# A two-layer decoder trunk on one core: six chunks transposed by VectorE instead of TensorE, and a new order of the first loads

## The chip, the cores and the metric

The kernel runs on one NeuronCore of a Trainium2 chip. The core has a matrix engine (TensorE, PE in the profile, with its weight loads as PEld), a vector engine (VectorE, DVE), an activation engine (ScalarE, ACT), a general engine (GpSimd, POOL) and a queue engine (SyncE, SP). SP, ACT and POOL issue DMA transfers. The metric is the device time of one execution in microseconds (us), the median of several.

## What is computed

The input x has 256 rows of 2048 floats. Two layers follow one another, each with a mixing half and a feed-forward half:

```python
h = rms_norm(x, mix_norm[l]);  proj = h @ w_in[l]          # q | k | v | u,v of the gating unit | gates
branch_a = sliding_window_attention(q, k, v, sinks[l]) @ w_attn_branch[l]
branch_b = chunked_sgu(gelu(uv), ...) @ w_sgu_branch[l]
x = x + (gates[:, :2048] * branch_a + gates[:, 2048:] * branch_b) @ w_out[l]
h2 = rms_norm(x, ffn_norm[l])
x = x + (silu(h2 @ w_gate[l]) * (h2 @ w_up[l])) @ w_down[l]     # inner width 5632
```

All arrays are 32-bit floats and the result has to keep that precision. The weights of both layers are read once.

## The kernel before, in words

**A product in three parts.** TensorE multiplies in a reduced format (fp32r). So each operand is split in a high part (a copy rounded to fp32r) and a low part (the value minus the high part), and a product is high x high + low x high + high x low. `Stream.split` (L217) does this for a weight tile: ACT writes `whi` (L225), DVE writes `wlo` (L226). `add_product` (L306) issues the matmuls (L314, L315).

**Weight stream.** The weights go through in entries. An entry is a tile `raw` of 256 rows by 512 columns (512 KB) for two blocks of 128 rows of x, twelve matmuls in all. SP loads the tiles (`Stream.load`, L196, L202; the first tile in two halves, L205) into five buffers, so a load waits until the tile five entries before has been split. Each of `whi` and `wlo` has four buffers. `Stream.next` (L230) asks for a tile up to seven entries ahead and splits up to four ahead (three in the first ten entries).

**Pairs.** Two column blocks that multiply the same x are taken together as a pair, in which one unit is multiplied with seven products in the place of eight (Winograd's form of Strassen). Its seven entries (tags P1 to P7, the head) are mixed with the last six entries of the pair before; for that some weight tiles are subtracted from one another on DVE (L213), and PSUM blocks are kept and joined (L336 to L342). A pair that follows a change of x is ordered by unit: all that uses unit 1, then unit 2, then unit 3.

**Units.** What stands on the left of a product has to be transposed: 512 columns of x (or of a hidden activation) become a unit, `uh` and `ul`, four 128x256 blocks each. `transposed` (L393) makes a unit, in one of two ways. With `on_pe`, TensorE transposes eight 128x128 blocks into PSUM (L425), and ACT and DVE split them from there (L411 and L416 with a scale, L407 and L408 without). Otherwise `turn` (L376) lets DVE transpose 32x32 blocks in place (L383, one instruction per 128 rows, into the tile `box`), and sixteen DMAs of 32 KB gather the blocks into a tile `tt` (L388); ACT and DVE split that one. The DMAs go out from POOL, or from SP where the caller says so.

**What sets the order.** TensorE's order is written by hand. After every two blocks `tick` (L246) counts a slot and runs what is due: `after(n, fn)` (L243) books fn n slots on. In `turn` the second transposition and the gathers come a slot after the first; in `transposed` the split comes six and seven slots on (plus `late`). DVE's instructions in a slot are kept behind the last `wlo` or subtraction (`tc.issue_after`). Beyond such bonds the order on DVE, ACT, POOL and SP is a planner's, which plays the program through with modelled durations.

**The places that the change touches.** `residual` (L849) adds a product to x and, where a norm follows, makes that norm's units (`nxt.unit`, L863) and sums of squares (L864); before, the last unit went over TensorE three slots on. `hidden` (L940) makes a chunk of the feed-forward activation; 11 chunks are done in rounds of 4, 4 and 3, and the last chunk of each round went over TensorE (L953, L954). `product_pair` (L368) calls both when a pair ends.

**The start.** SP loads x in chunks of 512 columns, two DMAs each (L258), with weight tiles between them as `LOAD_BY` (L49) says: tiles for 1, 3, 4 and 4 entries after chunks 1 to 4. POOL makes the identity and a mask, and loads small tables: `cs` and `sn` (L539, L540), `vrows` (L545 to L547), and `gn` and `snk` through `bcast` (L281). TensorE transposes all four units of the first norm, in slots 0, 1, 3 and 5. The squares of x (`Norm.squares`, L491, on ACT) are booked for slots 3 to 6 (L527), but the planner may put them earlier, since nothing binds them.

Of the kernel before, what the change touches and what calls it, by code (L numbers as in the profile page):

```python
# [45 lines left out]
Q_TURN = 7  # L46
Q_FIRST = 17
Q_STEP = 5
LOAD_BY = (1, 3, 4, 4)  # L49
FIRST_PART = [[(("kv", 0),), (("q", 0),)] + early + [(("v", 0),), (("v", 1),), (("gate", 1), ("u", 0)), (("u", 1), ("gate", 2)),  # L50
                                                  (("gate", 3), ("gate", 4))]
              for early in ([(("q", 1),), (("gate", 0),)], [(("q", 1), ("gate", 0))])]
# [5 lines left out]
def hybrid_trunk(ctx: ExitStack, tc: tile.TileContext, x, mix_norm, w_in, q_norm, k_norm, sinks,  # L58
# [129 lines left out]
    class Stream:  # L188
# [28 lines left out]
        def split(self, upto):  # L217
            while len(self.parts) < min(upto, len(entries)):
                e = entries[len(self.parts)]
                raw = self.raws[e["src"]]  # L220
                hi = wsp.tile([P, 2, CW], F32R, tag="hi", name=nm("whi"))
                lo = wsp.tile([P, 2, CW], F32R, tag="lo", name=nm("wlo"))
                one = len(self.parts) < 2
                for i in ([slice(0, 1), slice(1, 2)] if one else [slice(0, 2)]):
                    nc.scalar.activation(hi[:, i, :], raw[:, i, :], AF.Copy)  # L225
                    self.last = nc.vector.tensor_tensor(out=lo[:, i, :], in0=raw[:, i, :], in1=hi[:, i, :].bitcast(F32),  # L226
                                            op=ALU.subtract)
                self.parts.append((hi, lo))
# [49 lines left out]
    neg_half = const.tile([P, 24], F32, name="neg_half")  # L278
    nc.gpsimd.memset(neg_half, -0.5)

    def bcast(dst, row):  # L281
        nc.gpsimd.dma_start(dst, row.unsqueeze(0).to_broadcast([P, row.shape[0]]))


    def rsqrt(dst, src, n):
# [90 lines left out]
    def turn(dst, src, queue):  # L376


        box = turned.tile([P, 4, 4, NT, B], F32, tag="box", name=nm("box"))
        iv = src.rearrange("p t (k j c) -> p t k j c", j=4, c=B)  # L380

        def blocks(t):
            nc.vector.transpose(box[:, :, :, t, :].rearrange("p j k r -> p k j r"), iv[:, t])  # L383

        def gather():
            for j in range(4):
                for i in range(4):
                    queue.dma_start(dst[j * B:(j + 1) * B, i], box[i * B:(i + 1) * B, j])  # L388

        blocks(0)  # L390
        after(1, lambda: (blocks(1), gather()))

    def transposed(units, c, src, cols=None, on_pe=False, wino=None, again=False, queue=None, late=0):  # L393

        uh, ul = units[c] if again else (slot([P, 4, S], F32R, "uh"), slot([P, 4, S], F32R, "ul"))

        def view(ap):  # L400
            return ap.rearrange("p k (t i r) -> p (k t) i r", t=NT, r=B)

        def parts(k0, n, src_t):

            if cols is None:
                h, l, s_ = view(uh[:, k0:k0 + n, :]), view(ul[:, k0:k0 + n, :]), src_t(0, n)
                nc.scalar.activation(h, s_, AF.Copy)  # L407
                nc.vector.tensor_tensor(out=l, in0=s_, in1=h.bitcast(F32), op=ALU.subtract)  # L408
                return
            for k in range(n):  # L410
                nc.scalar.activation(view(uh[:, k0 + k:k0 + k + 1, :]), src_t(k, 1), AF.Copy,  # L411
                                     scale=cols[:, k0 + k:k0 + k + 1])
            for k in range(n):
                h, l, s_ = view(uh[:, k0 + k:k0 + k + 1, :]), view(ul[:, k0 + k:k0 + k + 1, :]), src_t(k, 1)
                for t in range(NT):
                    nc.vector.scalar_tensor_tensor(out=l[:, t], in0=s_[:, t], scalar=cols[:, k0 + k:k0 + k + 1],  # L416
                                                   in1=h[:, t].bitcast(F32), op0=ALU.mult, op1=ALU.subtract)

        if on_pe:
            for b in range(2):  # L420
                pt = ps_tr.tile([P, 2, S], F32, tag="tr", name=nm("pt"))
                for kk in range(2):
                    k = 2 * b + kk
                    for t in range(NT):
                        nc.tensor.transpose(pt[:, kk, t * P:(t + 1) * P], src[:, t, k * P:(k + 1) * P], ident)  # L425
                parts(2 * b, 2, lambda k, step, pt=pt: view(pt[:, k:k + step, :]))
            units[c] = (uh, ul)
            return

        tt = slot([P, 4, 4, NT, B], name="tt")  # L430
        turn(tt, src, queue or nc.gpsimd)

        def blocks_of(k0):
            return lambda k, step: tt[:, :, k0 + k:k0 + k + step].rearrange("p i k t r -> p (k t) i r")

        if not wino:
            def done():
                parts(2, 2, blocks_of(2))
                units[c] = (uh, ul)

            after(6 + late, lambda: parts(0, 2, blocks_of(0)))
            after(7 + late, done)
            return

        flat = {}

        def scaled(k0):

            if k0 == 0:
                flat["a"] = slot([P, 4, S], name="flat")  # L450
            for k in range(k0, k0 + 2):
                nc.scalar.activation(view(flat["a"][:, k:k + 1, :]), blocks_of(k)(0, 1), AF.Copy,
                                     scale=1.0 if cols is None else cols[:, k:k + 1])

        def split_(h, l, f):
            nc.scalar.activation(h, f, AF.Copy)
            nc.vector.tensor_tensor(out=l, in0=f, in1=h.bitcast(F32), op=ALU.subtract)

        def whole():
            if not again:  # L460
                split_(uh, ul, flat["a"])
                units[c] = (uh, ul)

        def sums(n):
            if n == 0:
                flat["s"] = slot([P, 4, 2, P], name="sums")
            ss = flat["s"]
            a11, a12, a21, a22 = (flat["a"][:, 2 * k:2 * k + 2, t * P:(t + 1) * P] for t in range(NT) for k in range(2))
            for o, x0, x1, op in ((0, a21, a22, ALU.add), (1, ss[:, 0], a11, ALU.subtract),
                                  (2, a11, a21, ALU.subtract), (3, a12, ss[:, 1], ALU.subtract))[2 * n:2 * n + 2]:  # L470
                nc.vector.tensor_tensor(out=ss[:, o], in0=x0, in1=x1, op=op)

        def finished():
            sh = slot([P, 4, 2, P], F32R, "sh")
            sl = slot([P, 4, 2, P], F32R, "sl")
            split_(sh, sl, flat["s"])
            units[c] = (uh, ul, sh, sl)

        for n, fn in zip(wino, (lambda: scaled(0), lambda: scaled(2), whole,
                                lambda: sums(0), lambda: sums(1), finished)):  # L480
            after(n, fn)

    class Norm:
# [10 lines left out]
                nc.scalar.activation(junk, xs[:, t, c * CW:(c + 1) * CW], AF.Square,  # L494
                                     accum_out=self.ss[t][:, c:c + 1])

        def unit(self, c, on_pe=False, again=False):
            transposed(self.units, c, xs[:, :, c * CW:(c + 1) * CW], cols=self.cols[:, 4 * c:4 * c + 4],
                       on_pe=on_pe, again=again,
                       wino=None if c != WINO or on_pe else WINO_FIRST if again else WINO_IN if self.soon else  # L500
                       WINO_NORM)

# [20 lines left out]
    after(1, lambda: norm.unit(1, True))  # L523
    after(3, lambda: norm.unit(2, True))
    after(5, lambda: norm.unit(3, True))
    for c in range(NCH):
        after(3 + c, lambda c=c: norm.squares(c))  # L527
    after(7, lambda: norm.finish())
    after(10, lambda: norm.unit(WINO, again=True))

# [5 lines left out]
                            compare_op=ALU.is_ge, fill=-1e30)  # L536
    cs = const.tile([P, NT, HD // 2], F32, name="cs")
    sn = const.tile([P, NT, HD // 2], F32, name="sn")
    nc.gpsimd.dma_start(cs, cosine.rearrange("(t p) h -> p t h", p=P))  # L539
    nc.gpsimd.dma_start(sn, sine.rearrange("(t p) h -> p t h", p=P))  # L540

    NB = DEPTH * D // P
    NV = 2 * NB + DEPTH * G
    vrows = const.tile([NV, P], F32, name="vrows")
    nc.gpsimd.dma_start(vrows[:NB, :], mix_norm.rearrange("l (k p) -> (l k) p", p=P))  # L545
    nc.gpsimd.dma_start(vrows[NB:2 * NB, :], ffn_norm.rearrange("l (k p) -> (l k) p", p=P))
    nc.gpsimd.dma_start(vrows[2 * NB:, :], b_spatial.rearrange("l g i -> (l g) i"))  # L547
    vcols = const.tile([P, NV], F32, name="vcols")

    def mix_cols(l):  # L550
# [298 lines left out]
    def residual(key, nxt=None, scale=1.0, store=False):  # L849

        def chunk(j, sums):
# [8 lines left out]
                        eng = nc.sync if i == 0 else nc.scalar  # L860
                        eng.dma_start(out[0, t * P:(t + 1) * P, sl], xs[:, t, sl])
            if nxt is not None:
                after(3 if j == NCH - 1 and not nxt.soon else 2, lambda: nxt.unit(j, j == NCH - 1 or j > 0 and nxt.soon))  # L863
                after(3, lambda: nxt.squares(j))  # L864
                if j == NCH - 1:
                    after(4, lambda: nxt.finish())
# [3 lines left out]
        return nxt  # L870

    prepare(0)

    for l in range(DEPTH):

# [64 lines left out]
        def hidden(hT, c):  # L940
# [8 lines left out]
            def on_up(up):  # L949
                for t in range(NT):  # L950
                    nc.vector.scalar_tensor_tensor(out=hid[:, t, :], in0=up[t], scalar=norm.rr[t], in1=hid[:, t, :],
                                                   op0=ALU.mult, op1=ALU.mult)
                pe = c == len(hT) - 1  # L953
                after(3 if pe else 2, lambda: transposed(hT, c, hid, on_pe=pe, wino=WINO_HID if c == WINO else None))  # L954

            product_pair(("ffn", l), on_gate, on_up)

# [49 lines left out]
```

## Time and profile before

| | us |
|---|---|
| three executions: median (lowest to highest) | 2474.78 (2472.15 to 2475.66) |
| the profiled execution, its own time | 2473.06 |
| its span in the trace | 2471.1 |
| TensorE busy | 2456.6 |
| DVE, ACT, POOL busy | 1925.3, 1430.8, 283.2 |

The span runs from the first instruction of the program to its last. Each row of a timeline gives the start, the duration, the engine, the line of the kernel, the operation, what it writes and reads (out<-in, by the program's names), how many were merged (x), and in brackets how long the engine had been idle and what ended that. Rows of `source` views give the count and the minimum, median and maximum duration in ns. PE's durations overlap with the next instruction's, so its pace is read from the starts. In the rows of waits stand the sum, the number and the longest one, in us. In the tables of stretches each engine has its busy time and its instructions (x); then come the granted clock of TensorE, the busy share of the DMA engines and the GB/s that they moved.

### The profile page before, as it was taken

The numbers are of one execution on the slowest core, as the hardware profiler recorded it, in microseconds if no ns is written. First come the engines' busy times: TensorE is split into PE (matmuls) and PEld (weight loads), VectorE is DVE, ScalarE is ACT, GpSimd is POOL, SyncE is SP. The second block draws the span as 40 slices with busy tenths as digits, with TensorE's granted clock in tenths as the row PEclk, the third lists the DMA queues.
The fourth block names the chain that finished last, engine by engine and source line by source line (L and its number), as shares of the span: only waits on it lengthen the run. The fifth ranks groups of instructions, "written<-read, shape, count | busy, mean of one in ns | idle before, by whom it ended". The sixth has DMA issues, their size and how long they took to land.

```text
span 2471.1 us, 31179 instructions
## 1 busy us (share of the span) xinstructions
PE 2456.6 (99%) x11088; PEld 2032.1 (82%) x11088; DVE 1925.3 (78%) x2261; ACT 1430.8 (58%) x1794; POOL 283.2 (11%) x527
## 2 busy tenths in 40 slices
PE   9999999999999999999999999999999999999999
PEld 7888888888888888888887888888888888888887
DVE  6798676887877787778887986767878777877786
ACT  5566544575655565556655665545655555655564
POOL 3100002231110111011101000021211001110110
PEclk9999999999999999999999999999999999999999
DMA  9655667576766667576757546666767566666664
GB/s 293 203 181 163 214 200 218 182 241 190 220 197 204 214 195 223 175 228 188 227 153 265 154 155 224 208 209 188 231 188 233 189 215 195 218 198 202 213 196 148
DMA packets 275662, 502.54 MB, mean 203 GB/s; under 512 B 26225, under 2 KB 36049, under 8 KB 275505
## 3 DMA queue, kind: packets, MB, share of 16 engines
q1 hardware_dynamic: 259472, 484.25, 61.8%
q0 software_dynamic: 15712, 16.01, 2.2%
q8 instruction: 87, 1.43, 0.2%
q14 instruction: 71, 0.57, 0.1%
q10 hardware_dynamic: 320, 0.27, 0.0%
HBM read 475.27 MB, written 2.10 MB: 193 GB/s over the span
## 4 chain that ended last, share of the span: by engine, by line
PE 94%; DVE 2%; DMA 1%; SPq 1%; issue 1%; ACT 0%; POOL 0%; DVEq 0%; ACTq 0%
PE acc L314 61%; PE acc L315 30%; DMA raw<-in_w_in_dram 1%; SPq L388 1%; DVE wlo L226 1%; PE po L762 1%; PE pt L425 1%; PE ppt L752 0%; PE psc L723 0%; ACT whi L225 0%; PE psg L840 0%; DVE box L383 0%; POOL rq L286 0%; DVE raw L213 0%; DVE gate L928 0%
## 5 line engine op out<-in xcount | busy, mean ns | idle before, releaser
L226 DVE TENSOR_TENSOR wlo<-raw,whi 128x1024 fp32r<-128x1024 f32 (+1 forms) x1039 | 1260.7, 1219 | 493.7 <-ACT whi L225 485.1
L225 ACT ACTIVATE whi<-raw 128x1024 fp32r<-128x1024 f32 (+1 forms) x1039 | 1098.2, 1058 | 919.4 <-PE acc L315 720.9
L314 PE MATMUL acc<-whi,uh 128*128 128x512 f32 x3114 | 1217.9, 391 | 1.2 <-ACT uh L411 1.2
L314 PE MATMUL acc<-wlo,uh 128*128 128x512 f32 x3114 | 1214.0, 390 | 2.2 <-DVE wlo L226 2.2
L315 PE MATMUL acc<-whi,ul 128*128 128x512 f32 x3114 | 1213.5, 390 | 0.0
L314 PEld LDWEIGHTS acc<-wlo,uh 128*128 128x128 f32 x3114 | 585.1, 188 | 124.9 <-DVE wlo L226 5.0
L314 PEld LDWEIGHTS acc<-whi,uh 128*128 128x128 f32 x3114 | 585.1, 188 | 121.7 <-ACT uh L411 1.8
L315 PEld LDWEIGHTS acc<-whi,ul 128*128 128x128 f32 x3114 | 584.9, 188 | 121.7 <-DVE ul L416 0.2
L388 POOL DMA_DIRECT2D tt<-box x480 | 235.2, 497 | 1714.9 <-DVE box L383 784.1
L213 DVE TENSOR_TENSOR raw<-raw,raw 128x1024 f32<-128x1024 f32 x188 | 229.2, 1219 | 1.3
L314 PE MATMUL acc<-whi,sh 128*128 128x512 f32 x376 | 147.3, 392 | 0.0
L314 PE MATMUL acc<-wlo,sh 128*128 128x512 f32 x376 | 147.1, 391 | 0.0
L315 PE MATMUL acc<-whi,sl 128*128 128x512 f32 x376 | 146.5, 390 | 0.0
L315 PEld LDWEIGHTS acc<-whi,sl 128*128 128x128 f32 x376 | 70.6, 188 | 14.7
L314 PEld LDWEIGHTS acc<-wlo,sh 128*128 128x128 f32 x376 | 70.7, 188 | 14.6 <-DVE kept L339 0.4
L314 PEld LDWEIGHTS acc<-whi,sh 128*128 128x128 f32 x376 | 70.7, 188 | 14.3
L339 DVE TENSOR_TENSOR kept<-acc,kept 128x512 f32<-128x512 f32 x94 | 64.2, 684 | 0.0
L342 ACT ACTIVATE acc<-kept 128x512 f32<-128x512 f32 x94 | 55.1, 587 | 10.8 <-DVE kept L339 10.7
L857 DVE SCALAR_TENSOR_TENSOR xs<-acc,xs 128x512 f32<-128x512 f32 (+1 forms) x66 | 41.4, 666 | 7.8 <-PE acc L315 7.8
L946 ACT ACTIVATE hid<-acc,rhalf 128x512 f32<-128x512 f32 x44 | 30.4, 690 | 21.0 <-PE acc L315 21.0
L947 DVE SCALAR_TENSOR_TENSOR hid<-hid,acc 128x512 f32<-128x512 f32 x44 | 29.6, 683 | 8.3 <-ACT hid L946 8.3
L336 ACT ACTIVATE kept<-acc 128x512 f32<-128x512 f32 x47 | 28.0, 597 | 13.2 <-PE acc L315 13.2
(135 smaller groups left out, 880.5 us busy)
## 6 DMA issues: line engine op xcount, KB each, us to landing
raw<-in_w_in_dram SPq DMA_DIRECT2D x239, 512.0 KB, 4.7
raw<-in_w_up_dram SPq DMA_DIRECT2D x176, 512.0 KB, 4.8
raw<-in_w_gate_dram SPq DMA_DIRECT2D x176, 512.0 KB, 4.3
raw<-in_w_down_dram SPq DMA_DIRECT2D x176, 512.0 KB, 4.6
raw<-in_w_out_dram SPq DMA_DIRECT2D x64, 512.0 KB, 4.8
raw<-in_w_attn_branch_dram SPq DMA_DIRECT2D x32, 512.0 KB, 5.3
raw<-in_w_sgu_branch_dram SPq DMA_DIRECT2D x32, 512.0 KB, 4.3
tt<-box POOLq DMA_DIRECT2D x480, 32.0 KB, 4.2
```

Of the source, the lines that this page charges most:

```text
L213: self.last = nc.vector.tensor_tensor(out=self.raws[d], in0=self.raws[x], in1=self.raws[y], op=ALU.subtract)
L225: nc.scalar.activation(hi[:, i, :], raw[:, i, :], AF.Copy)
L226: self.last = nc.vector.tensor_tensor(out=lo[:, i, :], in0=raw[:, i, :], in1=hi[:, i, :].bitcast(F32), op=ALU.subtract)
L314: nc.tensor.matmul(ps, a, part[:, kk, :], start=first and kk + n == 0, stop=False, skip_group_check=True)
L315: nc.tensor.matmul(ps, b, hi[:, kk, :], start=False, stop=kk == 1, skip_group_check=True)
L336: nc.scalar.activation(p.kept[:, 1, :], a[0], AF.Copy)
L339: nc.vector.tensor_tensor(out=p.kept[:, int(tag == "P7"), :], in0=a[1], in1=p.kept[:, 1, :], op=ALU.add)
L342: nc.scalar.activation(ps, p.kept[:, t, :], AF.Copy)
L388: queue.dma_start(dst[j * B:(j + 1) * B, i], box[i * B:(i + 1) * B, j])
L857: nc.vector.scalar_tensor_tensor(out=xs[:, t, sl], in0=sums[t][:, i * w:(i + 1) * w], scalar=scale, in1=xs[:, t, sl], op0=ALU.mult, op1=AL ...
L946: nc.scalar.activation(th, g[t], AF.Tanh, scale=norm.rh[t])
L947: nc.vector.scalar_tensor_tensor(out=th, in0=th, scalar=1.0, in1=g[t], op0=ALU.add, op1=ALU.mult)
```

## The change

There are four parts.

1. **Six chunks.** The fourth unit of the feed-forward norm (two layers) and the fourth hidden chunk in the two rounds of four (two layers) are turned by DVE and gathers, and no longer by TensorE. Their turning begins one slot after the pair's end, the split comes two slots earlier than for other turned chunks (`late=-2`), and the gathers alternate between SP and POOL. The third hidden chunk of the round of three, the last chunk of the mixing branch and the units of the two first norms stay on TensorE.
2. **First tiles.** `LOAD_BY` puts two weight tiles behind the first chunk of x, two behind the second and one behind the third.
3. **Held loads.** A copy of one column on POOL waits for the second half of x's third chunk, and the small tables are loaded by POOL after it. The loads of `vrows` move behind `prepare(0)`.
4. **First high part and squares.** The first half of the first weight tile gets its high part from DVE. The squares of x at the start come behind ACT's last weight split booked by then.

```diff
-LOAD_BY = (1, 3, 4, 4)
+LOAD_BY = (2, 4, 5, 5)
...
-                    nc.scalar.activation(hi[:, i, :], raw[:, i, :], AF.Copy)
+                    if not self.parts and i.start == 0:
+                        nc.vector.tensor_copy(hi[:, i, :], raw[:, i, :])
+                    else:
+                        self.high = nc.scalar.activation(hi[:, i, :], raw[:, i, :], AF.Copy)
...
+    held = const.tile([P, 1], F32, name="held")
+    hold = nc.gpsimd.tensor_copy(held, xs[:, 1, 2 * CW:2 * CW + 1])
+
+    def later(dst, src):
+        with tc.issue_after(hold.ins):
+            nc.gpsimd.dma_start(dst, src)
+
     def bcast(dst, row):
-        nc.gpsimd.dma_start(dst, row.unsqueeze(0).to_broadcast([P, row.shape[0]]))
+        later(dst, row.unsqueeze(0).to_broadcast([P, row.shape[0]]))
...
-                    queue.dma_start(dst[j * B:(j + 1) * B, i], box[i * B:(i + 1) * B, j])
+                    q = queue if queue is not None else (nc.sync, nc.gpsimd)[i % 2]
+                    q.dma_start(dst[j * B:(j + 1) * B, i], box[i * B:(i + 1) * B, j])
...
-    def transposed(units, c, src, cols=None, on_pe=False, wino=None, again=False, queue=None, late=0):
+    def transposed(units, c, src, cols=None, on_pe=False, wino=None, again=False, queue=nc.gpsimd, late=0):
...
+    def squared(c):
+        with tc.issue_after(stream.high.ins):
+            norm.squares(c)
+
     for c in range(NCH):
-        after(3 + c, lambda c=c: norm.squares(c))
+        after(3 + c, lambda c=c: squared(c))
...
-    nc.gpsimd.dma_start(cs, cosine.rearrange("(t p) h -> p t h", p=P))
-    nc.gpsimd.dma_start(sn, sine.rearrange("(t p) h -> p t h", p=P))
+    later(cs, cosine.rearrange("(t p) h -> p t h", p=P))
+    later(sn, sine.rearrange("(t p) h -> p t h", p=P))
...
-    nc.gpsimd.dma_start(vrows[:NB, :], mix_norm.rearrange("l (k p) -> (l k) p", p=P))
-    nc.gpsimd.dma_start(vrows[NB:2 * NB, :], ffn_norm.rearrange("l (k p) -> (l k) p", p=P))
-    nc.gpsimd.dma_start(vrows[2 * NB:, :], b_spatial.rearrange("l g i -> (l g) i"))
+
+    def rows():
+        later(vrows[:NB, :], mix_norm.rearrange("l (k p) -> (l k) p", p=P))
+        later(vrows[NB:2 * NB, :], ffn_norm.rearrange("l (k p) -> (l k) p", p=P))
+        later(vrows[2 * NB:, :], b_spatial.rearrange("l g i -> (l g) i"))
...
-                after(3 if j == NCH - 1 and not nxt.soon else 2, lambda: nxt.unit(j, j == NCH - 1 or j > 0 and nxt.soon))
+                last = j == NCH - 1 and not nxt.soon
+                after(1 if last else 2, lambda: nxt.unit(j, j > 0 and nxt.soon, queue=None if last else nc.gpsimd,
+                                                         late=-2 if last else 0))
...
     prepare(0)
+    rows()
...
-                pe = c == len(hT) - 1
-                after(3 if pe else 2, lambda: transposed(hT, c, hid, on_pe=pe, wino=WINO_HID if c == WINO else None))
+                pe, soon = c == len(hT) - 1 == 2, c == 3
+                after(3 if pe else 1 if soon else 2,
+                      lambda: transposed(hT, c, hid, on_pe=pe, wino=WINO_HID if c == WINO else None,
+                                         queue=None if soon else nc.gpsimd, late=-2 if soon else 0))
```

`Norm.unit` passes `queue` and `late` on to `transposed`, and `turn` is called with the queue as it is given.

More of the change, by code (lines that the diff above doesn't have):

```diff
@@ L430, in transposed @@
         tt = slot([P, 4, 4, NT, B], name="tt")
-        turn(tt, src, queue or nc.gpsimd)
+        turn(tt, src, queue)
         def blocks_of(k0):
@@ L495, in squares, with unit @@
                                      accum_out=self.ss[t][:, c:c + 1])
-        def unit(self, c, on_pe=False, again=False):
+        def unit(self, c, on_pe=False, again=False, queue=nc.gpsimd, late=0):
             transposed(self.units, c, xs[:, :, c * CW:(c + 1) * CW], cols=self.cols[:, 4 * c:4 * c + 4],
-                       on_pe=on_pe, again=again,
+                       on_pe=on_pe, again=again, queue=queue, late=late,
                        wino=None if c != WINO or on_pe else WINO_FIRST if again else WINO_IN if self.soon else
```

## The prediction

> **What bounds the kernel now.** I read the page first, then the list of waits of TensorE (PE), then its timeline around one of the changed places and in the first 33 us.
>
> ```profile
> span 2471.1 us, 31179 instructions
> PE 2456.6 (99%) x11088; PEld 2032.1 (82%) x11088; DVE 1925.3 (78%) x2261; ACT 1430.8 (58%) x1794; POOL 283.2 (11%) x527
> ```
> ```profile
> PE pt L425 <- DVE gate L928: 2.9, 2, 1.4
> PE acc L314 <- DVE wlo L226: 2.2, 5, 0.6
> ```
>
> PE is busy in all but 14.5 us of the span, and its longest sum of waits is 2.9 us, at a place that the change leaves alone (L928). So only two things can shorten the span: instructions that leave PE, and the few waits at the start. What lies on other engines costs nothing as long as the tiles arrive before PE asks for them.
>
> **Part one: six chunks leave PE.** The first fence is PE's timeline at one of them, then the sum row of a table of six stretches (one round each chunk, this line alone), then the row of the instruction.
>
> ```profile
> 549.97 0.39 PE L315 MATMUL acc<-whi,ul 128*128 128x512 f32 x1
> 550.20 1.04 PE L425 MATMUL pt<-ident,xs 128*128 128x128 f32 x8
> 550.99 0.48 PE L314 MATMUL acc<-whi,uh 128*128 128x512 f32 x1
> 551.30 0.40 PE L314 MATMUL acc<-wlo,uh 128*128 128x512 f32 x1
> ```
> ```profile
> sum 23.00, PE 6.21 PEld 5.60; mean PE 1.04 PEld 0.93
> ```
> ```profile
> L425 PE MATMUL pt<-ident,hid x48: 269/273/273, 719.7 to 2418.0; 128*128 128x128 f32 x48
> ```
>
> The busy column overlaps with what follows, so I go by starts. Matmuls start 0.23 us apart (549.97 to 550.20). Eight transposes take from 550.20 to 550.99, 0.79 us, and the next gap is 0.31 in place of 0.23: 0.87 us a chunk. The six chunks are unit 3 of the feed-forward norm (two layers) and the fourth hidden chunk of rounds one and two (two rounds, two layers); all six look alike (6.21 in sum, 1.04 each). Removed: 48 matmuls, **6 x 0.87 = 5.2 us**.
>
> The Trainium skill, "TensorE: Matmul & The Clock Gate", Part 4, gives about 275 ns for a transpose in a kernel's context and says that it does not count as PE-busy for the clock. By that figure 48 would be worth 13.2 us. The trace has the same 273 ns as a duration, but starts eight of them within 0.79 us, and I go by the starts.
>
> What replaces them: two 32x32-block transposes on VectorE (DVE) and 16 gathers a chunk, eight on SP and eight on GpSimd (POOL).
>
> ```profile
> L383 DVE STREAM_TRANSPOSE box<-hid x32: 700/704/705, 593.1 to 2372.6; 128x512 f32<-128x512 f32 x32
> ```
> ```profile
> L388 POOL DMA_DIRECT2D tt<-box x480: 496/496/567, 45.4 to 2382.8; - x160
> L388 SPq DMA_DIRECT2D tt<-box x192: 507/588/1383, 88.2 to 1548.6; - x192
> ```
> ```profile
> tt<-box POOLq DMA_DIRECT2D x480, 32.0 KB, 4.2
> tt<-box SPq DMA_DIRECT2D x192, 32.0 KB, 1.9
> ```
> ```profile
> 551.41 1.69 ACT L411 ACTIVATE uh<-tt,vcols 128x256 fp32r<-128x256 f32 x4
> 553.01 1.53 ACT L411 ACTIVATE uh<-pt,vcols 128x256 fp32r<-128x256 f32 x4
> ```
>
> DVE gets 6 x 2 x 0.70 = 8.4 us more, hidden in its idle fifth of the span. ScalarE (ACT) splits the same data from SBUF instead of PSUM, 1.69 against 1.53 us: hidden too. The gathers take 8 x 0.496 + 4.2 = 8.2 us on POOL and, beside it, 8 x 0.588 + 1.9 = 6.6 us on SP.
>
> Do they arrive in time? One slot is two blocks, twelve matmuls of 0.23, 2.7 us. Counted from the end of the pair, the code now puts the first transpose at slot 1 (at once), the second and the gathers at 2, the split at 5 and 6. The following pair takes its entries unit by unit, so that unit 3 is first used after slot 10 (nine slots on: half a one each for the last head entry and P3, eight whole ones). Data complete at slot 2 plus 8.2 us is slot 5: ACT may stand a slot at the split, and four slots, 11 us, are left before PE asks. While ACT stands, the weight tiles behind it wait; how far they can is in the rows below. POOL's reciprocal root of the norm's finish queues behind eight gathers (4.0 us), and is first needed at the end of the first feed-forward gate product, ten slots on. One more 4 KB slot is taken per chunk; counting the code's live tiles I get at most 23 of 25.
>
> **SP, past which the gathers are moved.** All weight loads queue behind eight gathers, which wait for DVE.
>
> ```profile
> ACT whi L225 <- PE acc L315: 720.9, 650, 4.4
> ```
> ```profile
> DMA to landing us min/median/max: 3.4/4.7/10.2
> ```
> ```profile
> 14.84 1.23 DVE L226 TENSOR_TENSOR wlo<-raw,whi 128x1024 fp32r<-128x1024 f32 x1 [2.57 <-ACT whi L225]
> ```
> ```profile
> 13.74 1.06 ACT L225 ACTIVATE whi<-raw 128x1024 fp32r<-128x1024 f32 x1 [2.28 <-DMA raw<-in_w_in_dram]
> ```
>
> ACT's splits mostly wait for PE to give back one of four buffers (720.9 us in 650 waits), so they run three entries ahead of need. Five raw tiles at 2.7 us an entry make 13.6 us from asking to splitting; less 4.7 for the landing and 2.3 for a split (1.06 + 1.23), 6.6 us are free. After that the three entries ahead, 8.2 less 2.3, give 5.9. Together 12.5 us may pass before PE stands. The gathers hold SP for 4.7 us after at most a slot and a transpose of waiting (3.4): 8.1 us. I cost this at **0**. The trace has a harder case: sixteen gathers in a row on SP, in the chain, with PE's busy time of the stretch.
>
> ```profile
> 64.03 0.60 SPq L388
> ...
> 73.53 0.59 SPq L388
> ```
> ```profile
> 60.00:100.00 40.00, 40.00 (x178) 33.13 (x178) 29.86 (x34) 20.68 (x25) 9.09 (x4) 1.00 0.59 188
> ```
>
> SP is held for ten microseconds there, and PE is busy in all 40 us.
>
> **Part two: the start.** PE's timeline, then ACT's, DVE's, POOL's and the stretches with DMA rate in the last column.
>
> ```profile
> 7.48 0.51 PE L314 MATMUL acc<-whi,uh 128*128 128x512 f32 x1 [1.24 <-ACT uh L411]
> ...
> 9.61 0.50 PE L314 MATMUL acc<-wlo,uh 128*128 128x512 f32 x1 [0.63 <-DVE wlo L226]
> ...
> 15.22 0.50 PE L314 MATMUL acc<-whi,uh 128*128 128x512 f32 x1
> 16.12 0.50 PE L314 MATMUL acc<-wlo,uh 128*128 128x512 f32 x1 [0.40 <-DVE wlo L226]
> ...
> 29.61 0.50 PE L314 MATMUL acc<-wlo,uh 128*128 128x512 f32 x1 [0.45 <-DVE wlo L226]
> ```
> ```profile
> 6.43 0.63 ACT L225 ACTIVATE whi<-raw 128x512 fp32r<-128x512 f32 x1 [0.48 <-DMA raw<-in_w_in_dram]
> 6.97 0.82 ACT L411 ACTIVATE uh<-pt,first_cols 128x256 fp32r<-128x256 f32 x2
> ```
> ```profile
> 8.87 0.68 DVE L226 TENSOR_TENSOR wlo<-raw,whi 128x512 fp32r<-128x512 f32 x1
> ```
> ```profile
> 1.60 0.87 POOL L539 DMA_DIRECT2D cs<-in_cosine_dram  x1
> ...
> 6.32 0.56 POOL L282 DMA_DIRECT2D snk<-in_sinks_dram  x1
> ```
> ```profile
> 10.00:12.00 2.00, 2.00 (x13) 1.66 (x12) 1.61 (x5) 1.41 (x4) 0.00 (x0) 1.00 0.89 162
> 12.00:20.00 8.00, 7.60 (x40) 6.02 (x39) 4.79 (x11) 6.25 (x15) 0.00 (x0) 1.00 1.04 396
> ```
> ```profile
> L623 DVE COPY wsT<-pw x4: 678/680/683, 127.8 to 1353.8; 128x512 f32<-128x512 f32 x4
> L559 DVE COPY vcols<-pv x1: 201/201/201, 44.5 to 44.5; 128x80 f32<-128x80 f32 x1
> ```
>
> *First high part.* At 6.43 ACT splits the first weight half and only then the unit (6.97), for which PE waits. With the copy on DVE the unit no longer queues, and the first matmul can go at 6.43 plus the copy. No SBUF-to-SBUF copy of 128x512 stands in the trace: it lies between 0.20 (128x80) and 0.68 (128x512, but from PSUM); I take 0.68, the same shape and operation. Then PE starts some 0.3 us earlier, but DVE's chain to the low part that ends at 9.55 (8.87 + 0.68) begins at 7.11 instead of 7.06, and PE meets it at 9.6 as before: gain 0, or 0.4 with the short copy.
>
> The Trainium skill, "VectorE: DVE Perf Modes", the perf-mode tier table, has fp32 SBUF copies at twice the rate, from which I estimate 0.42 us; by it the sum would be 0.3 us lower. No row here shows it.
>
> *Order of need and held loads.* The third tile lands at 13.74, ACT having stood 2.28 us, and its low part starts at 14.84; PE loses 16.12 - 15.22 - 0.23 = 0.67 us. From 10 to 12 us the DMA moves 162 GB/s, against 396 after, with the packets of POOL's eight small loads (issued 1.60 to 6.88) in the rings: 2 us at 234 KB/us less make 0.47 MB, 1.2 us at 396, lost to the weights. The new hold sends them behind the third chunk of x, when the tiles are ahead. The third tile then lands by about 12.5, before PE's need at 15. Gain **0.7 us**, plus 0.2 for the first tiles' earlier landing. x's second chunk moves behind the second tile, 0.5 MB or some 1.4 us later, but PE reaches its transposes only after twelve matmuls, so I cost that at 0; at worst it gives back the 0.7.
>
> *Squares wait.* The 16 square instructions leave ACT's early gaps.
>
> ```profile
> L494 ACT ACTIVATE junk<-xs 128x512 f32<-128x512 f32 x8 | 5.0, 634 | 1.8 <-DMA xs<-in_x_dram 1.8
> ```
> ```profile
> 20.00:36.00 16.00, 15.20 (x70) 11.98 (x69) 12.10 (x42) 9.82 (x16) 0.00 (x0) 1.00 0.90 326
> ```
>
> 5.0 us (more with the accumulator reads) come to a stretch of 16 us in which ACT is busy 9.8: it fits, barely. Behind them on ACT are the splits whose low part PE already awaits at 29.61 (0.45). I cost it at 0; bounds: all of that wait goes (-0.5), or the squares that don't fit are paid (+1.5).
>
> **Sum.** -5.2 - 0.9 = -6.1 us. The profiled execution took 2473.06 (span 2471.1 and 2.0 around it), 1.7 below the median 2474.78; the mean of the four times shown is 2473.9. I set the sum against that mean: **2467.8**. About 0.2%, 4.9 us, is what a measurement of this kernel can tell from no change.
>
> **Rivals.**
> - *ACT is the bound of the start.* The squares crowd out the splits before 36 us: part two costs 1.5 instead of giving 0.9. For: the 9.82 + 5.0 of 16. 2473.9 - 5.2 + 1.5 = 2470.2, chance 0.15.
> - *All of the start's waits go*, with the short copy and the wait at 29.61: 0.4 + 0.5 more, 2466.9 or a little less; 0.10.
> - *Slower: SP holds the weights.* If each SP gather waits for an earlier transfer, as the longest row (1.383 us) did, SP is held 8 x 1.383 + 3.4 = 14.5 us, 2.0 over the 12.5 that PE is covered for. 6 x 2.0 = 12 us against 6.1: 2479.8. It decides from 12.5 us of hold; at 13.5 a place it eats the gain. Against: the ten microseconds at 64 to 74. Chance 0.08.
> - *The change doesn't do what it says*: the planner lets DVE's transposes or the gathers slip, and PE waits for unit 3 about as long as it transposed. 2473; 0.09.
> - *A transpose is worth its 273 ns*: 2473.9 - 13.1 - 0.9 = 2459.9; 0.02.
>
> **How the numbers follow.** The forecast has 0.56. Faster: 0.56 + 0.10 + 0.02 = 0.68; within 0.2%: 0.15 + 0.09 = 0.24; slower: 0.08. The range of 8 in 10 takes the forecast, the first two rivals and most of the fourth, and leaves out the third and the last: 2463 to 2473.5.
>
> **What would show it.** PE's count falls by 48 to 11040. In the six places matmuls follow each other every 0.23 us without a wait, DVE's box transposes rise by twelve, and ACT stands under 3 us for gathered tiles. At the start ACT's wait for the third tile (2.28) and PE's 0.40 at 16.12 are gone, and the POOL loads come after 12 us. Wrong would be: PE waiting for unit 3 or for low parts just behind the six places, weight tiles landing after ACT is ready there, or PE gaps between 17 and 36 us that grow beyond 1.1.

## The result, and the profile after

| | before | after |
|---|---|---|
| median (lowest to highest), 22 runs each | 2472.8 (2471.43 to 2476.25) | 2469.8 (2468.43 to 2472.78) |
| ratio, 95% interval | | 0.9987 (0.9982 to 0.9993) |
| the profiled execution, its span | 2473.06, 2471.1 | 2468.67, 2467.0 |

The change takes 3.0 us off, half of the 6.1 that the sum gave. That is less than the 0.2% that the prediction called the limit of such a measurement, though the interval leaves out 1. The page of the kernel after begins so:

```profile
span 2467.0 us, 31322 instructions
PE 2452.7 (99%) x11040; PEld 2027.6 (82%) x11040; DVE 1932.5 (78%) x2274; ACT 1431.0 (58%) x1793; POOL 309.3 (13%) x576
```

PE has the 48 instructions less. Its list of waits has no new entry for a turned chunk:

```profile
PE pt L436 <- DVE gate L949: 2.9, 2, 1.4
PE ppt L770 <- DVE wsT L641: 2.3, 1, 2.3
PE acc L324 <- DVE wlo L229: 1.8, 5, 0.6
```

**The six places.** PE's timeline where the eight transposes stood (550 us):

```profile
549.99 0.39 PE L324 MATMUL acc<-whi,uh 128*128 128x512 f32 x1
550.22 0.39 PE L324 MATMUL acc<-wlo,uh 128*128 128x512 f32 x1
550.44 0.39 PE L325 MATMUL acc<-whi,ul 128*128 128x512 f32 x1
550.67 0.39 PE L324 MATMUL acc<-whi,uh 128*128 128x512 f32 x1
```

The starts are 0.22 to 0.23 us apart, with nothing between. I then numbered the product matmuls of both traces and took the start of the k-th after less that before. This difference falls by 0.88 at each of the six places, 5.3 in all, and rises again at none of them. The work went where it was meant to go, by the tile views of the turned chunks:

```profile
L393 DVE STREAM_TRANSPOSE box<-hid x40: 701/704/709, 592.7 to 2368.2; 128x512 f32<-128x512 f32 x40
L399 SPq DMA_DIRECT2D tt<-box x240: 507/588/1752, 89.0 to 2204.4; - x120
```

**The start.** Here the same difference has four parts. The first two show in the timelines of DVE, ACT and PE:

```profile
6.45 0.43 DVE L226 CAST whi<-raw 128x512 fp32r<-128x512 f32 x1 [5.37 <-DMA raw<-in_w_in_dram]
6.79 0.17 DVE L279 COPY first_cols<-pf 128x16 f32<-128x16 f32 x1
```
```profile
7.05 0.84 ACT L422 ACTIVATE uh<-pt,first_cols 128x256 fp32r<-128x256 f32 x2 [4.29 <-DVE first_cols L279]
...
11.69 1.06 ACT L228 ACTIVATE whi<-raw 128x1024 fp32r<-128x1024 f32 x1 [1.51 <-DMA raw<-in_w_in_dram]
```
```profile
7.58 0.50 PE L324 MATMUL acc<-whi,uh 128*128 128x512 f32 x1 [0.91 <-ACT uh L422]
...
10.30 0.63 PE L325 MATMUL acc<-whi,ul 128*128 128x512 f32 x1
10.72 0.63 PE L324 MATMUL acc<-whi,uh 128*128 128x512 f32 x1
11.15 0.63 PE L324 MATMUL acc<-wlo,uh 128*128 128x512 f32 x1
```

- *A new queue on DVE.* The small copy of `first_cols`, ready at 5.2 us, stands in DVE's order behind the new cast, which waits for the weight tile. ACT's unit needs `first_cols`. So the first product goes at 7.58 in place of 7.48: +0.1.
- *Half clock.* From 9.60 to 13.01 us the trace's clock record has 0.5 (the row of 10 to 12 us below has it as well) and the matmuls stand 0.43 apart: +1.5. The profiled execution of before has no such window. Of the fourteen profiled executions (two of after, one of each other kernel) twelve have one or two such windows, most of them at 8 to 14 us or behind PE's wait for `wsT` near 1350. After itself has one in the first execution and two in the second, three kernels that differ from before by an unread tile alone have one, and the kernel with all start edits and no turned chunks has none. So I take them to come with the execution and not with the change; how often each kernel has them was not measured.
- *The third tile.* It reaches ACT at 11.69 in place of 13.74, and PE's wait at 16.12 is gone: -0.84, where 0.7 was forecast.
- *The held loads* go out from 14.55 to 18.81 us:

```profile
14.55 0.89 POOL L289 DMA_DIRECT2D cs<-in_cosine_dram  x1
...
18.81 0.50 POOL L289 DMA_DIRECT2D vrows<-in_b_spatial_dram  x1
```
```profile
10.00:12.00 2.00, 2.00 (x5) 1.52 (x5) 1.89 (x5) 0.49 (x2) 0.00 (x0) 0.50 1.05 401
18.00:26.00 8.00, 8.00 (x42) 6.66 (x41) 4.40 (x10) 4.22 (x11) 1.31 (x3) 1.00 1.05 349
```

The table of stretches has the GB/s last. The weights now have 401 from 10 to 12 us (162 before), and 349 from 18 to 26. Before, that row was:

```profile
18.00:26.00 8.00, 8.00 (x46) 6.80 (x44) 5.79 (x12) 5.21 (x12) 0.00 (x0) 1.00 1.05 406
```

The 0.48 MB gained in the first stretch (239 x 2) are paid back in the second (57 x 8, 0.46 MB). It is the held loads that take it: a kernel of the experiments that has them, but whose packets are as fast as in before (hold in `table`), has 354 there:

```profile
18.00:26.00 8.00, 8.00 (x44) 6.74 (x44) 3.86 (x10) 3.78 (x10) 1.79 (x4) 1.00 1.05 354
```

A wait of PE behind it stays as it was (0.45 before):

```profile
30.33 0.51 PE L324 MATMUL acc<-wlo,uh 128*128 128x512 f32 x1 [0.46 <-DVE wlo L229]
```

**Where the second layer starts** something appears that no step of the forecast had:

```profile
1331.11 0.50 PE L324 MATMUL acc<-wlo,uh 128*128 128x512 f32 x1 [0.34 <-DVE wlo L229]
```

PE waits for weights there, and the difference rises by 0.5. Each packet of 2,048 bytes, as the weights come in, has its duration in the trace. In before nearly all take 84 ns; in after, where the DMA engines are saturated, many take 87 to 97 ns, and these are the slow packets below: 35% between 1280 and 1360 us (0% before).

### The profile page after: what moved, and what is told of

Its sections match the earlier page's. It is cut to its first block, busy times and chain, and to the rows that moved or that the text cites. A ratio compares the mean times of both kernels' runs of the same rounds, so it can differ in the third digit from the quotient of the medians.

```text
span 2467.0 us, 31322 instructions
## 1 busy us (share of the span) xinstructions
PE 2452.7 (99%) x11040; PEld 2027.6 (82%) x11040; DVE 1932.5 (78%) x2274; ACT 1431.0 (58%) x1793; POOL 309.3 (13%) x576
## 4 chain that ended last, share of the span: by engine, by line
PE 95%; DMA 2%; DVE 2%; SPq 1%; ACT 0%; issue 0%; POOL 0%; DVEq 0%; ACTq 0%
PE acc L324 61%; PE acc L325 31%; DMA raw<-in_w_in_dram 2%; DVE wlo L229 1%; PE po L780 1%; SPq L399 1%; PE psc L741 0%; PE ppt L770 0%; PE pt L436 0%; ACT whi L228 0%; PE psg L858 0%; POOL rq L296 0%; DVE box L393 0%; DVE ul L427 0%; DVE raw L213 0%
## 5 line engine op out<-in xcount | busy, mean ns | idle before, releaser
L399 POOL DMA_DIRECT2D tt<-box x528 | 259.6, 499 | 1710.2 <-DMA raw<-in_w_up_dram 503.6
L419 DVE TENSOR_TENSOR ul<-tt,uh 128x512 fp32r<-128x512 f32 x52 | 34.0, 685 | 2.9 <-ACT uh L418 2.9
```

Of the source, the lines that this page charges most:

```text
L399: q.dma_start(dst[j * B:(j + 1) * B, i], box[i * B:(i + 1) * B, j])
```

## The experiments

All were timed in five rounds, each group on one chip beside before, to which its ratios refer. My theory at first was that the chunks carry the gain and the start is held back by a wait; its rivals are in the expectations, where the letters belong to each text.

**Each half alone.** The first kernel has only the six chunks (the edits of parts two to four undone), the second only the start (the chunks back on TensorE).

> Only the first part of the change: the six chunks are turned by VectorE, with gathers from two queues; first tiles, small loads, first high part and squares as before. Theory A (the six chunks give their whole 5.2 us, and the rest of the change takes some back at the start): 5 us below the kernel before, ratio 0.998, below the whole change by about 2 us, and no longer waits of TensorE than before. Rival B (the turned chunks give back part, by late tiles or held weight loads): 3 us below, ratio 0.9988, like the whole change, with new gaps of TensorE behind the six places.

2467.41 against 2473.41, 0.9975 (0.9966 to 0.9984): -6.0. The chunks alone give the forecast of the whole.

> Only the other parts: order of the first tiles, held small loads, first high part by VectorE, squares bound; the six chunks stay on TensorE. Theory A: 1 to 2.5 us above the kernel before, ratio 1.0004 to 1.001, with the first scale copy behind the first high part on VectorE, the first unit at about 7.05 us on ScalarE, and in many executions a stretch of 3.4 us at half clock before 14 us. Rival B: 0.9 us below (the start as predicted), ratio 0.9996.

2475.56, 1.0008 (0.9999 to 1.0017): +2.2. The start, forecast to gain 0.9, shows no gain and more likely costs (the interval just reaches 1). Its trace has no half clock, so that part of my theory is not the reason. In this trace PE is 0.75 us ahead of before at the 36th product, 0.15 behind at the 120th, and loses another 0.9 at 1334 us; 39% of its packets there are slow. The kernel with the chunks alone has 0%.

**DVE's order, and a warmer clock.** Both start from after:

```diff
-    nc.vector.tensor_copy(first_cols, pf[:, :16])
+    cols_made = nc.vector.tensor_copy(first_cols, pf[:, :16])
...
-                        nc.vector.tensor_copy(hi[:, i, :], raw[:, i, :])
+                        with tc.issue_after(cols_made.ins):
+                            nc.vector.tensor_copy(hi[:, i, :], raw[:, i, :])
```

The second kernel has, besides, two matmuls on the tile `warm` behind the first unit's transposes:

```diff
     norm.unit(0, True)
+    for i in range(2):
+        nc.tensor.matmul(pw_, warm, warm, start=True, stop=True)
```

> The whole change, but VectorE has to copy the first scale columns before it makes the first high part. Theory A: the first unit's high part starts at about 5.8 us instead of 7.05, the first product at about 6.95 instead of 7.58; at least 0.5 us below the whole change, and up to 2 us if TensorE's busier start also keeps the clock from being halved. Rival (the half clock depends on the phase of its window alone): first product earlier, but at most 0.3 us faster in the median and half clock in as many executions.

> As the run before it, with two warm-up products more (128x128, result not used) between TensorE's first transposes and the first product, about 0.85 us of work in a gap. If idle time before the first products halves the clock: no half clock between 5 and 16 us in the profile, and 0.5 us or more faster than without them; if not, the same or up to 0.4 us slower, since they reach into the first product's time.

2470.40 (0.9988, 0.9979 to 0.9997) and 2470.54 (0.9988, 0.9979 to 0.9997): a miss, no faster than after. The first product does come earlier, at 6.87 and 7.23, and in the first of the two PE is 1.50 us ahead of before at the 48th product. Its timeline shows where that went:

```profile
28.61 0.50 PE L325 MATMUL acc<-whi,uh 128*128 128x512 f32 x1 [1.18 <-ACT whi L229]
29.87 0.50 PE L325 MATMUL acc<-wlo,uh 128*128 128x512 f32 x1 [0.76 <-DVE wlo L230]
```

Near 29 us PE has caught up with the weights, so whatever it gained earlier it waits for there. Neither profiled execution has half clock ahead of 16 us, with the two matmuls or without, so whether they keep the clock up stays open.

**The tile `held`.** From 40 us on, the engines' order of work in the start alone is that of before, so no order explains the packets there. What the change adds besides is a tile: 128x1, 4 bytes a partition, for which the allocator sets 32 aside. In the compiled programs the five raw buffers, to which the weights are loaded, start at byte 141,056 of a partition in before and in the chunks alone, and at 141,088 in after and the start alone. The next four kernels test this: after with the hold's copy put into an unread old tile; before with 32 and with 64 unread bytes; and the first again with DVE's order mended.

```diff
-    held = const.tile([P, 1], F32, name="held")
-    hold = nc.gpsimd.tensor_copy(held, xs[:, 1, 2 * CW:2 * CW + 1])
+    hold = nc.gpsimd.tensor_copy(table, xs[:, 1, 2 * CW:2 * CW + 1])
```
```diff
     nc.gpsimd.memset(neg_half, -0.5)
+    held = const.tile([P, 1], F32, name="held")
+    nc.gpsimd.memset(held, 0.0)
```

> The kernel after, but the hold's copy writes into the one-column tile table, which nothing reads, so that the new tile held is not there and every later tile lies 32 bytes lower: raw tiles start at 141,056 bytes of a partition, as before, in place of 141,088. All instructions and waits are those of after. Theory A (the 32 bytes slow the weight transfers: packets of 2,048 bytes at 88 to 96 ns in place of 84 while the DMA is saturated): share of packets between 87 and 97 ns back to under 3% in every stretch, PE's wait for wlo at about 1331 us at most 0.2 in place of 0.5, 1 to 2.5 us faster than after, 2467.3 to 2468.8. Rival B (the order of the loads and the wait of the squares cost it by themselves): same packets and the same 2469.8 as after.

2467.98 against 2473.84, 0.9975 (0.9965 to 0.9984): -5.9. The packets are back at 84 ns.

> The kernel before with one more tile of 128x1 (4 bytes a partition, of which 32 are set aside) behind neg_half, set to zero once by POOL and read by nothing; no part of the change is in it. Raw tiles start at 141,088. Theory A: 10 to 40% of the weight packets in the saturated stretches take 88 to 96 ns, PE waits 0.5 to 1 us more at about 1331 us, 1 to 2.5 us slower than before, ratio 1.0004 to 1.0010. Rival B: the same time as before, packets at 84 ns.

2477.25, 1.0013 (1.0004 to 1.0022): +3.4, from a tile that nothing reads, and more than expected. Its packets between 1280 and 1360 us are slow by 37%. Its rate from 18 to 26 us, with the loads and the order of before, and its waits at the second layer's start:

```profile
18.00:26.00 8.00, 8.00 (x41) 6.72 (x40) 6.73 (x16) 5.96 (x13) 0.00 (x0) 1.00 1.05 385
```
```profile
1334.54 0.50 PE L316 MATMUL acc<-whi,uh 128*128 128x512 f32 x1 [0.73 <-ACT whi L225]
1335.80 0.50 PE L316 MATMUL acc<-wlo,uh 128*128 128x512 f32 x1 [0.76 <-DVE wlo L226]
```

385 GB/s in place of 406, with the DMA engines as busy (1.05).

> As the kernel with 32 bytes more, but the unread tile is 128x16 (64 bytes a partition): raw tiles start at 141,120, a multiple of 64 again, though not of 128. Theory A in its form that a multiple of 64 is what counts: packets at 84 ns and the time of before within 0.5 us. Theory A in its form that a multiple of 128 counts, or that any shift does it: packets at 88 to 96 ns and 1 to 2.5 us slower. Rival B: the same time as before.

2477.45, 1.0013 (1.0004 to 1.0022): +3.6, 35% slow. A multiple of 64 is not enough.

> The kernel after with the hold in table, and the first high part on VectorE issued behind the copy of first_cols. Theory A: first product at 6.9 in place of 7.5 us, packets at 84 ns, and 0 to 0.6 us faster than the kernel with the hold in table alone, 2466.8 to 2468.5. Rival C (what the start gains is lost again in one of the waits up to 36 us, for PE takes the tiles faster than they land): no faster than the kernel with the hold in table alone.

2467.64, 0.9973 (0.9962 to 0.9985): -6.2, the same as with the hold in `table` alone. The weight came only after 6.7 us in its profiled execution, so its first product went at 7.31. PE is 0.92 us ahead of before at the 36th product, almost exactly the 0.9 forecast for the start, and 0.20 ahead at the 120th:

```profile
29.36 0.50 PE L324 MATMUL acc<-wlo,uh 128*128 128x512 f32 x1 [0.76 <-DVE wlo L230]
```

**Which addresses.** The last four are after once more; after with `held` made 128x32, of which the copy still writes one column; before with 128 unread bytes; and before with only the raw buffers moved, by 32 bytes ahead of them and 96 behind:

```diff
+    pool_a = ctx.enter_context(tc.tile_pool(name="pool_a", bufs=1))
     wraw = ctx.enter_context(tc.tile_pool(name="wraw", bufs=5))
+    pool_b = ctx.enter_context(tc.tile_pool(name="pool_b", bufs=1))
...
+    held = pool_a.tile([P, 1], F32, name="held")
+    nc.gpsimd.memset(held, 0.0)
+    rest = pool_b.tile([P, 24], F32, name="rest")
+    nc.gpsimd.memset(rest, 0.0)
```

> The kernel after, unchanged, timed beside the three that follow. Both theories: 2.5 to 4 us faster than before (2469.8 was measured), packets between 87 and 97 ns at 25 to 40% in the stretch from 1280 to 1360 us.

2470.80 against 2474.14, 0.9986 (0.9978 to 0.9995), as in the first measurement.

> The kernel after with the tile held made 128x32 (128 bytes a partition), of which the hold's copy still writes one column: the same instructions, and raw tiles start at 141,184, a multiple of 128 as in before. Theory A in the form that raw tiles off a multiple of 128 bytes slow the weight transfers: packets between 87 and 97 ns under 3%, PE's wait at about 1331 us at most 0.2, and 1.5 to 3 us faster than the kernel after beside it, 2467 to 2468.3. Theory A2 (any shift from the place of before does it): no faster than after, packets at 88 to 96 ns. Rival B (part two's order costs it, and the fast kernel with the hold in table was luck of its run): the time of after.

2470.63, 0.9984 (0.9975 to 0.9993): a miss for the multiple of 128, no faster than after.

> The kernel before with one unread tile of 128x32 (128 bytes a partition), set to zero once by POOL. Raw tiles start at 141,184, a multiple of 128. Theory A: the time of before within 1 us and packets at 84 ns. Theory A2 (any shift): 3 to 4 us slower, as with 32 and with 64 bytes more. If the new POOL instruction itself were the cost: 3 to 4 us slower with packets at 84 ns.

2476.39, 1.0011 (1.0002 to 1.0020): +2.3, a miss as well; 33% of the packets are slow.

> The kernel before with 32 unread bytes directly ahead of the five raw buffers and 96 directly behind them: only the raw tiles start off a multiple of 128 (141,088); all that lies ahead is where it was, and all behind is moved by 128 bytes. Theory A (where the weight transfers write is what counts): 3 to 4 us slower than before and 20 to 40% of the packets at 87 to 97 ns, as with 32 bytes ahead of everything. If it is the tiles that the engines read and write (whi, wlo, tt, box) that lost by the shift: the time of before.

2530.64, 1.0229 (1.0215 to 1.0243): +56.5, a miss for both. 27% of its packets are slow, though nothing that lies ahead of the raw buffers moved, neither x nor the units. So what lies ahead is not needed for the effect. But the run was laid out with a shift by 128 as the harmless one, and the kernel with 128 bytes shows that it is not. So this run does not part the raw buffers, moved by 32, from the tiles behind them, moved by 128. Its time is another matter, told at the end.

The kernels side by side; slow packets are those of 87 to 97 ns, and waits are what PE lost between product matmuls from 1300 to 1348 us in the profiled execution, half-clock windows left out. In the last row the raw buffers moved by 32 bytes and what lies behind them by 128:

| kernel | raw buffers start | over a multiple of 256 | slow packets, 1280 to 1360 us | waits, us | against before, us |
|---|---|---|---|---|---|
| before | 141,056 | 0 | 0% | 0.38 | |
| chunks alone | 141,056 | 0 | 0% | 0.11 | -6.0 |
| hold in `table` | 141,056 | 0 | 0% | 0.11 | -5.9 |
| the same, columns first | 141,056 | 0 | 0% | 0.11 | -6.2 |
| after, after beside | 141,088 | 32 | 35%, 38% | 0.72, 1.23 | -3.0, -3.3 |
| after, `held` of 128 bytes | 141,184 | 128 | 33% | 0.74 | -3.5 |
| columns first, without and with the two matmuls | 141,088 | 32 | 37%, 35% | 1.26, 1.32 | -3.0, -2.9 |
| start alone | 141,088 | 32 | 39% | 1.12 | +2.2 |
| before and 32 bytes | 141,088 | 32 | 37% | 2.14 | +3.4 |
| before and 64 bytes | 141,120 | 64 | 35% | 1.56 | +3.6 |
| before and 128 bytes | 141,184 | 128 | 33% | 2.37 | +2.3 |
| before, raw buffers moved | 141,088 | 32 | 27% | 0 | +56.5 |

Where a kernel has a twin without the shift (before, the hold in `table`, or the same with columns first), the shift costs 2.3 to 3.6 us in the medians; the last row is a case of its own. The intervals are some 2 us to either side. Each kernel without a shift has fast packets. The traces place a part of that cost. I compared the starts of the k-th product again, leaving out the half-clock windows. The three kernels that add a tile to before lose 0.3 to 1.1 us up to 300 us and 1.2 to 2.0 from 1300 to 1348 us, where a layer starts and PE waits for weights. From 300 to 1300 us and behind 1450 us they lose at most 0.07. The rest of the cost is not placed: one execution of each was profiled, and each of these three has a window of half clock, 0.7 to 1.7 us, which the one of before has not. Whether longer waits for weights make such windows more frequent is open.

The Trainium skill, "DMA: Bandwidth & Descriptors", "How a descriptor splits into AXI transactions", says that a transaction has to start at a 256-byte boundary, so that a descriptor which starts off one begins at the boundary below and pays for bytes that it does not use. The page tells this of bytes that are fetched; here the shifted address is the one written to. As far as the boundary goes the runs are in line with it: 141,056 is 551 x 256, and none of the slow starts is a multiple of 256. By an estimate from the page's count of beats, 65, 66 and 68 in place of 64, a larger shift would cost more; here the slow share falls from 37 to 33% as the shift grows from 32 to 128, which the page does not explain. No run has a shift by 256, so that it is the multiple of 256, and not the old place, remains argued, and so does that the raw buffers alone are what counts.

The chunks alone and the hold in `table` are faster than before, and probably than after: 0.9975 (0.9966 to 0.9984) and 0.9975 (0.9965 to 0.9984) against 0.9987 (0.9982 to 0.9993), intervals that just overlap. With the start's edits or without them makes no difference that these runs can tell.

## Why the prediction was right or wrong

- **Transposes that leave PE, -5.2: right**, 5.3 in the trace, and 6.0 in the medians for the whole half alone (4.0 to 8.4 by the interval). The rule by starts held; 273 ns each would have made 13.
- **SP past the gathers, DVE's 8.4 us, ACT's split, all at 0: right.** PE waits for no turned chunk. ACT's waits for gathered tiles went from 17.4 + 8.1 to 18.9 + 7.7 us:

```profile
ACT qT L725 <- DMA tt<-box: 18.9, 4, 5.5
...
ACT uh L418 <- DMA tt<-box: 7.7, 4, 3.5
```

- **First high part, 0 or -0.4: wrong in its cause.** The cast took 0.43 us; I took 0.68. My estimate from the Trainium skill, "VectorE: DVE Perf Modes", the perf-mode tier table, was 0.42, and the trace agrees. The gain went to what the step did not name: the copy of `first_cols` queued behind the waiting cast on DVE. Mending that brings the first product to 6.87 (its weight came 0.3 earlier in that execution), and no time in the median.
- **Order of need and held loads, -0.9: the size right, the end wrong.** The third tile came as forecast (-0.84). But "when the tiles are ahead" failed: from 14 to 29 us they are not ahead, the held loads took their rate there, and PE, near 29 us, was as late as the weights. With packets at 84 ns the start is worth 0.2 us by 41 us (columns first against before) or 1.1 (hold in `table` against the chunks alone, whose half-clock window cost 0.9 more), and nothing that the medians can tell.
- **Squares, 0 with bounds -0.5 and +1.5: right.** PE's two gaps from 17 to 36 us were 0.45 and 0.35 and are 0.46 and 0.15.
- **The step that failed is the sum: a term was missing.** The hold was priced by its wait and its queue, and its tile at nothing. Its 4 bytes cost 2.3 to 3.6 us, as the pairs with and without a shift show; that they do so through the raw buffers and the packets is what the slow shares point to. Without them the time is 2467.98 and 2467.64 beside a before of 2473.84, or -5.9 and -6.2 where the sum gave -6.1. This nearness does not confirm every term: the chunks alone give -6.0, so the start's 0.9 is in no median.
- **That the time lies within 2463 to 2473.5 is luck.** The range was drawn for other rivals and reaches almost to the time of before; that it also holds a cost that nobody had named says nothing for the sum.
- Of the rivals none came true. The result lies where *ACT is the bound of the start* put it, 2470.2, but from another cause: ACT had time for the squares.

## What to carry to other kernels

Price the memory of a new tile too, not only its instructions: one of 4 bytes shifts every buffer allocated behind it, and if the weights' buffers leave a place at which their packets are fast, the stretches in which the kernel waits for transfers become longer. Compare the durations of the packets and the addresses before looking for the cause in the order of work. And a gain ahead of a stretch in which the transfers are the limit is given back at its end; measure it behind that stretch.

## What the hardware showed that was not expected

- A shift of the tiles, the weights' destination among them, by 32, 64 or 128 bytes slows a part of the 2,048-byte packets from 84 to between 87 and 97 ns where the DMA engines are saturated (385 in place of 406 GB/s with 32 bytes). Not every busy stretch is slowed: in the three kernels that add a tile to before, 56 to 61% of the packets from 18 to 29 us are slow, but under 0.5% of those from 12 to 16 us, when loads of x are still among them and 366 to 368 GB/s are moved. Why is open.
- Windows of half clock last 3.41 us each and come and go with the execution (one and two in the two of after), costing 0.7 to 1.7 us. The Trainium skill, "TensorE: Matmul & The Clock Gate", Part 1, describes a free-running window of 4,096 cycles, 3,413 ns; the length agrees with the traces.
- With the raw buffers moved by 32 bytes and what lies behind them by 128, PE itself was slower, from end to end. Two groups of product matmuls on that kernel's page, then one on the page of before; the mean duration in ns stands ahead of the second bar:

```profile
L320 PE MATMUL acc<-whi,uh 128*128 128x512 f32 x3114 | 1233.8, 396 | 1.3 <-ACT uh L417 1.3
L320 PE MATMUL acc<-wlo,uh 128*128 128x512 f32 x3114 | 1230.1, 395 | 0.9 <-DVE wlo L228 0.9
```
```profile
L314 PE MATMUL acc<-wlo,uh 128*128 128x512 f32 x3114 | 1214.0, 390 | 2.2 <-DVE wlo L226 2.2
```

  Its timeline at one place:

```profile
547.91 0.39 PE L320 MATMUL acc<-whi,uh 128*128 128x512 f32 x1
...
550.00 0.40 PE L320 MATMUL acc<-whi,uh 128*128 128x512 f32 x1
```

  The nine starts between these rows are 0.232 us apart, against 0.227 elsewhere; 5 ns on 10,470 matmuls are 52 of the 57.6 us that its span grew. The granted clock is 0.999, transposes still start 109 ns apart, and in five stretches from 548 to 2300 us the mean step is 0.232 or 0.233 us. It is also the only kernel in which the weights' split tiles, which lie behind the raw buffers, moved by 128 bytes against the units that lie ahead of them. PE reads both; whether that is the cause was not tried.
